# Hybrid attention layer: six x tiles and three blocks of look-ahead in the output stage, a later value product in the local attention, a later request for the next head's bias

## The chip, the cores and the metric

One of the cores of a Trainium2 chip runs the whole kernel. The metric is the device time of one execution in microseconds, the median of three runs. The five engines are TensorE (PE; its weight loads are shown as a lane of their own, PEld), VectorE (DVE), ScalarE (ACT), GpSimd (POOL) and SyncE (SP). In this kernel SP issues every DMA, and it issues them in one order.

## The reference, cut to what matters

Two sequences, 1024 tokens (prompt) and 2048 tokens (sample), width 1024, float32, each go through the same layer:

```python
u = x * (1.0 + scale[:, None]) + shift[:, None]
qa, ka, va, ga, qb, kb, vb, gb = jnp.split(u @ w_in, SPLIT_OFFSETS, axis=-1)
oa = window_gqa(qa, ka, va, sink, rel_bias) * jax.nn.silu(ga)
ob = diff_attention(qb, kb, vb, lq1, lk1, lq2, lk2, subln_w, rel_bias, lambda_init) * jax.nn.silu(gb)
h = jnp.concatenate([oa, ob], axis=-1) @ w_out
return layer_norm(ALPHA * x + gate[:, None] * h, ln_g, ln_b)
```

`window_gqa` is the local attention: 8 heads, blocks of 128 queries, each against its own block of keys and the two beside it, with a bias by distance. `diff_attention` has 4 heads of two softmaxes each over all keys, again with a bias by distance, and takes one from the other.

## The kernel before, in words

A float32 product is made of three matmuls on rounded parts: high by high, high by low, low by high. Most products appear three times in the profile for that reason (L186 to L188, L864 to L866, L1037 to L1039); the local attention's logits and values take two.

The work runs in four stages, one after another on TensorE:

1. **Projections** (to about 669 us): `u` is built and multiplied by `w_in`. The results go to DRAM. A part of this work is kept back and used as filler beside the next stage.
2. **Local attention** (`windowed`, about 669 to 1080 us): 24 blocks, each in two halves `n` of four heads. `first(B, n)` makes the logits of a head per step (matmul L602, bias and minimum on DVE L604, exponential on ACT L607). `second(B, n)` is run two halves later: a step per key block `b`, with four transposes into one PSUM tile (L635), a rounded copy on ACT (`pthA`, L638) and the rest on DVE (`ptlA`, L639). The value product of key block `b` (L629 with `pthA`, L630 with `ptlA`) stands one step behind, right after the transposes of `b + 1`. The last step adds up and stores. A half has four steps, and in each of them, beside a step of `first` and a step of `second`, `beside()` takes some matmuls of the kept-back projections.
3. **Differential attention** (`slot`, about 1098 to 1870 us): units of 128 queries (256 for the prompt) with `logits`, `transpose` three units later, and `values`. The sample's heads have 16 units each. Each head has a bias tile `W` (128x2432), made by `load_head` from one DMA and two spreads on POOL (L752), and key tiles. They come from `Ring`s: buffers that are opened in two steps. For the first three units, while the projections' pool is still open, `W` has one buffer and the keys four; afterwards there are two and six. `prefetch` calls `load_head` for the next head at unit `i == 2` of a head, which for the first head is in the time of the small rings.
4. **Output** (`outputs`, about 1863 us to the end): 24 blocks of 128 tokens, the sample's 16 and then the prompt's 8. `load_rest(t)` asks for five pieces: `ot`, `frow`, `gb` and `oa` into one tile `d` (from `dat`), and the block's `x` (from `xts`). `join(t)` multiplies them (POOL L1006 and L1007) and splits the result in `oH` (ACT L1010) and `oL` (POOL L1011). `output` runs 48 matmuls of 512 columns (L1037 to L1039) into PSUM tiles `po` (four, two per block), then gate, residual and statistics on DVE (L1042 to L1052), the power on POOL (L1053), the scaling on ACT into the `x` tile (L1077), the addition on POOL (L1078), and the store of the `x` tile (L1079). `Views(make, n)` hands out `n` tiles in turn; here 3 for `x`, 2 for `d`, 2 for `oH`/`oL`. All of them are memory of the earlier stage: value tiles `vt`, rows `l`, query tiles `Q` and transposed tiles `pth`/`ptl`.

TensorE's order is the order of the program text (`manual_schedule`). The order on the other engines and on SP is set by a planner, which simulates the kernel and issues what is ready, and what has a free buffer, first. Each engine then keeps its order and waits in place.

Of the kernel before, what the change touches and what calls it, by code (L numbers as in the profile page):

```python
# [11 lines left out]
F32 = mybir.dt.float32  # L12
F32R = mybir.dt.float32r
AF = mybir.ActivationFunctionType
ALU = mybir.AluOpType
# [4 lines left out]
P = 128  # L20
# [46 lines left out]
def hybrid_layer(ctx, tc, x_prompt, x_sample, c_prompt, c_sample, w_in, w_out, w_ada, b_ada, ln_g, ln_b,  # L67
                 attn_sink, lambda_q1, lambda_k1, lambda_q2, lambda_k2, subln_w, rel_bias, oh, eye,
                 y_prompt, y_sample):
    nc = tc.nc  # L70
# [15 lines left out]
    def tp():  # L86
        return ps_tp.tile([P, 512], F32, tag="tp", name="tp")
# [20 lines left out]
    grow = dt_([2, D], "grow")  # L108
# [3 lines left out]
    ident = const.tile([P, P], F32, name="ident")  # L112
# [189 lines left out]
    done, pending = {}, []  # L302
# [230 lines left out]
    def windowed(upto):  # L533

        order = [(s, i) for s in (0, 1) for i in range(SEQS[s] // P)]
        NB = len(order)
        Bs, seconds, n0 = {}, [iter(()), iter(())], done.get(2, 0)
        total = (upto - n0) * 32
        Bs[0] = load_block(*order[0])
        count = [0, 0]  # L540

        def beside():
            count[0] += 1
            while count[1] * NB * 16 < count[0] * total and done.get(2, 0) < upto:
                next(steps, None)
                count[1] += 1

        for t in range(NB + 2):
            for n in range(2):
                if t < NB and order[t][0] == 1 and order[t][1] >= 7:  # L550
                    project_until(2, 5)
                f = first(Bs[t], n) if t < NB else iter(())
                for h4 in range(4):
                    next(f, None)
                    beside()
                    next(seconds[0], None)
                    beside()
                for _ in seconds[0]:
                    pass
                seconds = [seconds[1], second(Bs[t], n) if t < NB else iter(())]  # L560
                if n == 0 and t + 1 < NB:
                    Bs[t + 1] = load_block(*order[t + 1])
            Bs.pop(t - 1, None)
        project_until(2, upto)

    def load_keys_of(s, i):
# [53 lines left out]
    def second(B, n):  # L620

        nb, l = B["nb"], B["l"][n]
        O = ac()
        parts = []

        def values(b):
            H, L = parts[b]
            v = B["V"][:, b, n * P:(n + 1) * P]
            nc.tensor.matmul(O, lhsT=v, rhs=H, start=(b == 0), stop=False)  # L629
            nc.tensor.matmul(O, lhsT=v, rhs=L, start=False, stop=(b == nb - 1))  # L630

        for b in range(nb):
            pt = tp()
            for h4 in range(4):
                nc.tensor.transpose(pt[:, h4 * P:(h4 + 1) * P], l[:, h4, 1 + b * P:1 + (b + 1) * P], ident)  # L635
            H = pa_p.tile([P, 512], F32R, tag="pth", name="pthA")
            L = pa_p.tile([P, 512], F32R, tag="ptl", name="ptlA")
            nc.scalar.copy(H, pt)  # L638
            nc.vector.tensor_tensor(out=L, in0=pt, in1=H.bitcast(F32), op=ALU.subtract)  # L639
            parts.append((H, L))  # L640
            if b:
                values(b - 1)
            yield
        values(nb - 1)
        if n == 0:
            B["og"] = og_p.tile([P, 4, P], F32, tag="og", name="og")
        og = B["og"]
        tmp = og_p.tile([HD, 2, 2, P], F32, tag="tmp", name="tmpA")
        nc.scalar.copy(tmp, O[HD:P, :].rearrange("p (j m q) -> p j m q", j=2, m=2))
        o4 = O[0:HD, :].rearrange("p (j m q) -> p j m q", j=2, m=2)  # L650
        for m in range(2):
            nc.vector.tensor_tensor(out=og[m * HD:(m + 1) * HD, 2 * n:2 * n + 2, :], in0=o4[:, :, m, :],
                                    in1=tmp[:, :, m, :], op=ALU.add)
        if n == 1:
            nc.gpsimd.tensor_tensor(out=og, in0=og, in1=B["G"], op=ALU.mult)
            s, cs = B["s"], slice(B["i"] * P, (B["i"] + 1) * P)
            nc.sync.dma_start(out=OA[s][:, :, cs].rearrange("i r t -> r i t"), in_=og)
        yield
# [10 lines left out]
    pa_p = pool(ast, "ptA", 3)  # L669
# [30 lines left out]
    class Views:  # L700
# [5 lines left out]
        def next(self):  # L706
            if len(self.made) < self.count:
                self.made.append(self.make())
            self.n += 1
            return self.made[(self.n - 1) % self.count]  # L710
# [8 lines left out]
    units, groups_of, values_at, sums_at = [], [], {}, {}  # L719
    for s in (1, 0):  # L720
        T = SEQS[s] // P
        for h in range(HB):
            for i in range(0, T, 2):
                g = len(groups_of)
                n = len(units)
# [7 lines left out]
    order = [(s, h) for s in (1, 0) for h in range(HB)]  # L733
# [41 lines left out]
    def prefetch(n, j):  # L775

        s, h, i, g = units[n]
        if n + 1 < N and j == 1 and g != units[n + 1][3]:
            load_queries(units[n + 1][3])
        if i == 2 and j == 2 and (s, h) != units[-1][:2]:  # L780
            load_head(*next_head[s, h])
        if n + 1 < N and units[n + 1][2] == 0 and j == 3:
            load_keys(*units[n + 1][:2], range(2, SEQS[units[n + 1][0]] // CH))
# [50 lines left out]
    def transpose(n, j):  # L834
# [5 lines left out]
        if b == 0:  # L840
            groups_[g]["PT"].append((pt_p.tile([P, 4, QG], F32R, tag="pth", name="pth"),
                                     pt_p.tile([P, 4, QG], F32R, tag="ptl", name="ptl")))
        H, L = groups_[g]["PT"][kq]
        pt = tp()
# [104 lines left out]
    def part():  # L949
        return weight(next(turn))  # L950
# [4 lines left out]
    def query():  # L955
        return q_p.tile([P, 2, 2, QG], F32R, name="Q").rearrange("p a m q -> p (a m q)")

    def value():
        return v_p.tile([P, 2, 4, P], F32R, tag="v", name="vt").rearrange("p h b e -> p (h b e)")

    os_ = Views(lambda: (query(), query()) if not os_.made else (part(), part()), 2)
    xts = Views(value, 3)
    dat = Views(row0, 2)
    woH, woL, keep, raws = {}, {}, {}, {}

    def stage(ks):
# [21 lines left out]
    def load_rest(t):  # L988

        s, i = order[t]  # L990
        cs = slice(i * P, (i + 1) * P)
        d = dat.next().rearrange("p (n i q) -> p n i q", n=4, i=4)
        nc.sync.dma_start(out=d[:, 1], in_=OT[s][:, :, cs].rearrange("k r t -> r k t"))
        nc.sync.dma_start(out=d[:, 2], in_=frow[s][:, cs].partition_broadcast(P))
        nc.sync.dma_start(out=d[:, 3], in_=GB[s][:, :, cs].rearrange("k r t -> r k t"))
        nc.sync.dma_start(out=d[:, 0], in_=OA[s][:, :, cs].rearrange("i r t -> r i t"))
        xt = xts.next().bitcast(F32)
        nc.sync.dma_start(out=xt, in_=xs[s][cs, :])
        Bs[t] = dict(s=s, i=i, d=d, xt=xt)

    def join(t):

        B = Bs[t]
        d = B["d"]
        B["oH"], B["oL"] = [v.rearrange("p (k q) -> p k q", k=KC) for v in os_.next()]
        nc.gpsimd.tensor_tensor(out=d[:, 1], in0=d[:, 1], in1=d[:, 2], op=ALU.mult)  # L1006
        nc.gpsimd.tensor_tensor(out=d[:, 1], in0=d[:, 1], in1=d[:, 3], op=ALU.mult)  # L1007
        for half in range(2):
            hs = slice(half * 4, half * 4 + 4)
            nc.scalar.copy(B["oH"][:, hs, :], d[:, half])  # L1010
            nc.gpsimd.tensor_tensor(out=B["oL"][:, hs, :], in0=d[:, half], in1=B["oH"][:, hs, :].bitcast(F32),  # L1011
                                    op=ALU.subtract)


    def load_gate(s):
        if "gate" not in keep:
            keep["gate"] = part().bitcast(F32)
        nc.sync.dma_start(out=keep["gate"], in_=grow[s, :].partition_broadcast(P))

    def load_norm():  # L1020
        for name, v in (("g", ln_g), ("b", ln_b)):
# [3 lines left out]
    def output(B, end):  # L1025

        s, cs = B["s"], slice(B["i"] * P, (B["i"] + 1) * P)
        gate, gbc, bbc = keep["gate"], keep["g"], keep["b"]
        xt, oH, oL = B["xt"], B["oH"], B["oL"]
        bs = sA_p.tile([P, 4, 6], F32, tag="bs", name="bs")  # L1030
        accs = []
# [49 lines left out]
    order = [(s, i) for s in (1, 0) for i in range(SEQS[s] // P)]  # L1081
    NB = len(order)
    Bs = {}

    def outputs():

        load_rest(0)
        stage((4, 5, 6, 7))
        yield
        for k in range(3):  # L1090
            split_weights(k)
            yield
        load_gate(order[0][0])
        load_norm()
        for k in range(3, 7):
            split_weights(k)
            yield
        split_weights(7)
        load_rest(1)
        join(0)  # L1100
        for t in range(NB):
            s, i = order[t]
            if i == 0 and t:
                load_gate(s)
            for j, _ in enumerate(output(Bs[t], t == NB - 1)):
                if j == 2 and t + 2 < NB:
                    load_rest(t + 2)
                if j == 8 and t + 1 < NB:
                    join(t + 1)
                yield  # L1110
            del Bs[t]
            yield
# [40 lines left out]
```

## Time and profile before

| what | value |
|---|---|
| median of 3 runs (lowest to highest) | 2234.81 us (2233.54 to 2236.45) |
| the profiled execution | 2232.28 us, its span 2230.5 us |
| mean granted TensorE clock | 0.981 of 2.4 GHz |
| TensorE busy, weight loads busy | 94%, 80% of the span |
| DVE, ACT, POOL busy | 59%, 46%, 52% |
| DMA, mean over the span | 140 GB/s |

The shares are means over stages that have different limits. The table shows TensorE nearly always busy; what can still change must be looked for stage by stage, in the time between one matmul's start and the next. "Idle before" in the rows below is the time in which an engine had nothing, and behind the arrow stands what ended it. PEclk is the granted clock as a share of 2.4 GHz.

### The profile page before, as it was taken

How to read it: one execution, taken by the hardware profiler on the slowest of the kernel's cores; microseconds unless marked ns; L12 is line 12 of the kernel's file. 1: busy time of each engine (PE TensorE's matmuls, PEld its weight loads, DVE VectorE, ACT ScalarE, POOL GpSimd, SP SyncE). 2: the span in 40 equal slices, each digit the busy share in tenths (PEclk: the TensorE clock that was granted, in tenths of full speed). 3: DMA queues.
4: the chain of work that ended last, by engine and by line, in shares of the span. 5: the costliest groups of instructions: out<-in, count | busy, mean ns of one | idle time of the engine just before them, and what ended most of it. 6: DMA issues, size and time to landing. Idle time of an engine off the chain costs nothing.

```text
span 2230.5 us, 32729 instructions
## 1 busy us (share of the span) xinstructions
PE 2104.7 (94%) x11597; PEld 1791.7 (80%) x11597; DVE 1307.5 (59%) x2538; ACT 1031.8 (46%) x2022; POOL 1153.5 (52%) x836
## 2 busy tenths in 40 slices
PE   7999999999999999999999999999999988678898
PEld 4777888888988788888978889999998877556676
DVE  6334124212246667667539889999999975333445
ACT  5211113111136666667327777777778973111111
POOL 3213123212133334433248878888988885455565
PEclk9999999999999999999999999999999998889999
DMA  9676536345359667786524221232315548444553
GB/s 276 179 264 178 158 128 183 114 132 146 129 164 241 162 168 190 192 220 156 155 77 130 78 74 39 79 82 78 76 44 128 114 100 162 97 131 135 151 178 113
DMA packets 340203, 312.46 MB, mean 140 GB/s; under 512 B 32086, under 2 KB 296950, under 8 KB 339656
## 3 DMA queue, kind: packets, MB, share of 16 engines
q1 hardware_dynamic: 340040, 310.37, 51.4%
q8 instruction: 92, 1.51, 0.4%
q14 instruction: 71, 0.58, 0.2%
HBM read 212.70 MB, written 97.60 MB: 139 GB/s over the span
## 4 chain that ended last, share of the span: by engine, by line
PE 41%; DMA 8%; issue 6%; POOL 4%; DVE 2%; ACT 1%; SPq 1%; POOLq 0%; DVEq 0%; ACTq 0%
PE lg L808 12%; PE tp L846 5%; PE ac L866 3%; PE ac L865 3%; PE ac L864 3%; DMA l<-ot 3%; PE pj L186 3%; PE pj L188 3%; PE pj L187 3%; DMA out<-vt 2%; DMA Q<-qb 2%; PE lgA L602 2%; PE tp L635 1%; PE ac L630 1%; POOL vt L1078 1%
## 5 line engine op out<-in xcount | busy, mean ns | idle before, releaser
L186 PE MATMUL pj<-uH,wH 128*128 128x512 f32 x1040 | 415.3, 399 | 5.3 <-DVE gg L257 5.3
L188 PE MATMUL pj<-uH,wL 128*128 128x512 f32 x1040 | 407.8, 392 | 0.0
L187 PE MATMUL pj<-uL,wH 128*128 128x512 f32 x1040 | 407.1, 391 | 0.0
L217 POOL TENSOR_TENSOR wL<-wr,wH 128x1024 fp32r<-128x1024 f32 x74 | 181.6, 2456 | 417.8 <-DVE wH L215 369.9
L808 PE MATMUL lg<-kt,Q 128*128 128x512 f32 x1280 | 380.0, 418 | 14.7 <-DVE nm L813 6.3
L832 POOL TENSOR_TENSOR l<-l,l 128x1024 f32<-128x1024 f32 x160 | 382.4, 2412 | 0.2
L821 ACT ACTIVATE l<-l,nm 128x2048 f32<-128x2048 f32 (+1 forms) x192 | 331.0, 1724 | 26.3 <-DVE nm L813 26.1
L808 PEld LDWEIGHTS lg<-kt,Q 128*128 128x128 f32 x1280 | 218.8, 191 | 48.2 <-issue 10.4
L813 DVE CUSTOM_DVE_ANT_0 l<-lg,W 128x1024 f32<-128x1024 f32 x192 | 233.3, 1215 | 21.2 <-PE lg L808 16.6
L830 POOL TENSOR_SCALAR l<-l,s 128x1024 f32<-128x1024 f32 x160 | 179.1, 1131 | 121.5 <-DVE s L826 52.3
L848 ACT CAST pth<-tp 128x512 fp32r<-128x512 f32 x320 | 186.1, 582 | 118.7 <-PE tp L846 115.0
L188 PEld LDWEIGHTS pj<-uH,wL 128*128 128x128 f32 x1040 | 195.7, 188 | 42.7
L186 PEld LDWEIGHTS pj<-uH,wH 128*128 128x128 f32 x1040 | 195.9, 188 | 38.5 <-DVE gg L257 6.1
L187 PEld LDWEIGHTS pj<-uL,wH 128*128 128x128 f32 x1040 | 196.0, 188 | 31.4
L849 DVE TENSOR_TENSOR ptl<-tp,pth 128x512 fp32r<-128x512 f32 x320 | 209.0, 684 | 16.9 <-ACT pth L848 15.7
L846 PE MATMUL tp<-ident,l 128*128 128x128 f32 x1280 | 195.5, 276 | 9.6 <-DVE ptl L849 9.5
L617 POOL TENSOR_SCALAR l<-l,rcA 128x384 f32<-128x384 f32 (+1 forms) x144 | 82.6, 592 | 202.8 <-DVE rcA L611 179.4
L864 PE MATMUL ac<-pth,vt 128*128 128x256 f32 x640 | 182.1, 285 | 2.9 <-ACT ac L881 2.9
L866 PE MATMUL ac<-pth,vt 128*128 128x256 f32 x640 | 183.1, 286 | 0.0
L865 PE MATMUL ac<-ptl,vt 128*128 128x256 f32 x640 | 182.5, 285 | 0.0
L813 DVE CUSTOM_DVE_ANT_0 l<-lg,W,nm 128x1024 f32<-128x1024 f32 x128 | 164.0, 1281 | 23.2 <-PE lg L808 16.1
L846 PEld LDWEIGHTS tp<-ident,l 128*128 128x128 f32 x1280 | 150.4, 142 | 12.6 <-DVE ptl L849 4.7
(206 smaller groups left out, 4071.7 us busy)
## 6 DMA issues: line engine op xcount, KB each, us to landing
wr<-in_w_in SPq DMA_DIRECT2D x39, 1024.0 KB, 5.6
KAt<-ka SPq DMA_DIRECT2D x40, 384.0 KB, 7.3
QAt<-qa SPq DMA_DIRECT2D x24, 512.0 KB, 5.6
kt<-kb SPq DMA_DIRECT2D x24, 512.0 KB, 6.6
Q<-qb SPq DMA_DIRECT2D x48, 256.0 KB, 3.2
Q<-qb SPq DMA_DIRECT2D x96, 128.0 KB, 4.0
vt<-vb SPq DMA_DIRECT2D x48, 256.0 KB, 6.9
out<-vt SPq DMA_DIRECT2D x23, 512.0 KB, 5.2
```

The source lines that it names most:

```text
L186: nc.tensor.matmul(acc, lhsT=a(k), rhs=b(k), start=(k == 0), stop=False)
L187: nc.tensor.matmul(acc, lhsT=a(k), rhs=bl(k), start=False, stop=False)
L188: nc.tensor.matmul(acc, lhsT=al(k), rhs=b(k), start=False, stop=(k == KC - 1))
L808: nc.tensor.matmul(L[:, c * CH:(c + 1) * CH], lhsT=G["Q"][:, v, m, b * P:(b + 1) * P], rhs=Kt[kt0 + c][:, m, :], start=(v == 0), stop=(v = ...
L813: nc.vector.tensor_tensor_reduce(out=half, in0=L, in1=W[:, off:off + 1024], scale=1.0, scalar=nm[:, m, 0:1] if s and hf else 3e38, op0=ALU ...
L821: nc.scalar.activation(e, e, AF.Exp, bias=nm[:, m, hf:hf + 1], scale=-1.0, accum_out=sums)
L832: nc.gpsimd.tensor_tensor(out=row[:, cs], in0=row[:, cs], in1=rows[n][1][:, cs], op=ALU.add)
L846: nc.tensor.transpose(pt[:, c * P:(c + 1) * P], rows[n][0][:, (j * 4 + c) * P:(j * 4 + c + 1) * P], ident)
L849: nc.vector.tensor_tensor(out=L[:, :, qs], in0=p3, in1=H[:, :, qs].bitcast(F32), op=ALU.subtract)
L864: nc.tensor.matmul(a, lhsT=Vt[kq][:, 0, c, :], rhs=H[:, c, :], start=(kb == 0), stop=False)
L865: nc.tensor.matmul(a, lhsT=Vt[kq][:, 0, c, :], rhs=L[:, c, :], start=False, stop=False)
L866: nc.tensor.matmul(a, lhsT=Vt[kq][:, 1, c, :], rhs=H[:, c, :], start=False, stop=(kb == T - 1))
```

## The change

Four edits in the output stage: six tiles for `x` instead of three, four for `d` instead of two, three pairs of `oH`/`oL` instead of two; `load_rest` runs three blocks ahead instead of two, and `join` is called at step 4 of the block before instead of step 8; the gate vectors of the two sequences get a tile each, and the second is asked for at block 8 instead of being loaded over the first at block 16. In the local attention the value product of key block `b` stands in front of the transposes of `b + 2`, so `second` has one more step than a half has, and two halves' generators can be alive at once. In the differential attention the next head is asked for at `i == 4` instead of 2 in the sample's heads.

```diff
-        Bs, seconds, n0 = {}, [iter(()), iter(())], done.get(2, 0)
+        Bs, live, wait, n0 = {}, [], [], done.get(2, 0)
@@ windowed
-                    next(seconds[0], None)
+                    for g in list(live):
+                        if next(g, live) is live:
+                            live.remove(g)
                     beside()
-                for _ in seconds[0]:
-                    pass
-                seconds = [seconds[1], second(Bs[t], n) if t < NB else iter(())]
+                if t < NB:
+                    wait.append(second(Bs[t], n))
+                if len(wait) > 1 or t >= NB and wait:
+                    live.append(wait.pop(0))
@@ second
-        for b in range(nb):
-            pt = tp()
...
-            if b:
-                values(b - 1)
-            yield
-        values(nb - 1)
+        for b in range(nb + 2):
+            if b > 1:
+                values(b - 2)
+            if b < nb:
+                pt = tp()
...
+            if b <= nb:
+                yield
@@ prefetch
-        if i == 2 and j == 2 and (s, h) != units[-1][:2]:
+        if i == (4 if s else 2) and j == 2 and (s, h) != units[-1][:2]:
             load_head(*next_head[s, h])
@@
-    os_ = Views(lambda: (query(), query()) if not os_.made else (part(), part()), 2)
-    xts = Views(value, 3)
-    dat = Views(row0, 2)
+    os_ = Views(lambda: (query(), query()) if not os_.made else (part(), part()), 3)
+    xts = Views(lambda: value() if len(xts.made) < 5 else part(), 6)
+    dat = Views(row0, 4)
@@ load_gate
-        if "gate" not in keep:
-            keep["gate"] = part().bitcast(F32)
-        nc.sync.dma_start(out=keep["gate"], in_=grow[s, :].partition_broadcast(P))
+        keep[s] = part().bitcast(F32)
+        nc.sync.dma_start(out=keep[s], in_=grow[s, :].partition_broadcast(P))
@@ outputs
         load_rest(1)
+        load_rest(2)
         join(0)
         for t in range(NB):
-            s, i = order[t]
-            if i == 0 and t:
-                load_gate(s)
+            if t == 8:
+                load_gate(0)
             for j, _ in enumerate(output(Bs[t], t == NB - 1)):
-                if j == 2 and t + 2 < NB:
-                    load_rest(t + 2)
-                if j == 8 and t + 1 < NB:
+                if j == 2 and t + 3 < NB:
+                    load_rest(t + 3)
+                if j == 4 and t + 1 < NB:
                     join(t + 1)
```

## Rows read from the trace of the kernel before

**Rows 1.** Busy time of the engines in stretches of the span: the local attention, the first head change, the entry to the output stage, its first 16 blocks and the later ones. Columns: length; busy us (instructions) of PE, PEld, DVE, ACT, POOL; granted clock; DMA share; GB/s.
```profile
669.00:1080.00 411.00, 398.71 (x2116) 330.40 (x2115) 278.40 (x719) 272.87 (x698) 153.37 (x185) 1.00 0.73 186
...
1165.00:1300.00 135.00, 125.28 (x805) 111.65 (x806) 115.84 (x219) 96.62 (x155) 103.26 (x65) 0.97 0.34 97
...
1833.00:1884.30 51.30, 39.97 (x241) 36.19 (x240) 31.04 (x52) 23.87 (x64) 31.98 (x25) 0.87 0.75 168
1884.30:2122.00 237.70, 183.79 (x720) 144.05 (x719) 88.15 (x150) 32.70 (x57) 117.01 (x105) 0.91 0.49 127
2122.00:2211.30 89.30, 82.56 (x339) 65.15 (x338) 40.83 (x70) 17.33 (x30) 58.07 (x51) 0.96 0.50 163
```

**Rows 2.** Who waited for whom from 1884.3 to 2211.3 us (blocks 1 to 22 of the output). Columns: who, for whom, us in total, times, the longest.
```profile
ACT vt L1077 <- POOL ve L1053: 272.6, 22, 19.7
...
POOL l L1006 <- DMA l<-ot: 147.2, 21, 14.1
...
PE po L1037 <- ACT vt L1077: 60.5, 18, 8.9
```

**Rows 3.** The same stretch, what SP's queue itself waited for (L998 loads x, L994 loads frow).
```profile
SPq L994 <- POOL l L1006: 111.5, 19, 11.1
...
SPq L998 <- DMA out<-vt: 51.8, 19, 5.7
```

**Rows 4.** POOL in order of time over one block. Columns: start, us, engine, line, operation, out<-in, count, idle before.
```profile
2043.51 1.29 POOL L1006 TENSOR_TENSOR l<-l 128x512 f32<-128x512 f32 x1 [7.58 <-DMA l<-ot]
2044.77 2.53 POOL L1078 TENSOR_TENSOR vt<-vt,pth 128x512 f32<-128x512 f32 x2
...
2058.66 1.28 POOL L1006 TENSOR_TENSOR l<-l 128x512 f32<-128x512 f32 x1 [7.14 <-DMA l<-ot]
```

**Rows 5.** SP's queue in order of time in the same block: the store, the x load and the ot load.
```profile
2047.32 0.35 SPq L1079 DMA_DIRECT2D out<-vt  x1
...
2054.08 0.35 SPq L998 DMA_DIRECT2D vt<-in_x_sample  x1
2054.52 0.39 SPq L993 DMA_DIRECT2D l<-ot  x1
```

**Rows 6.** TensorE in order of time: the first matmul of blocks 1, 22 and 23 of the output.
```profile
1884.32 0.39 PE L1037 MATMUL po<-kt,ptl 128*128 128x512 f32 x1
...
2200.15 0.50 PE L1037 MATMUL po<-kt,Q 128*128 128x512 f32 x1
...
2211.32 0.39 PE L1037 MATMUL po<-kt,ptl 128*128 128x512 f32 x1
```

**Rows 7.** Busy time in three shorter stretches: the wait ahead of block 2, blocks 17 and 18, block 22. Columns as in rows 1.
```profile
1884.30:1910.00 25.70, 17.47 (x68) 13.77 (x67) 9.66 (x17) 2.91 (x5) 6.81 (x8) 0.87 0.55 60
...
2137.00:2159.90 22.90, 22.70 (x98) 17.95 (x96) 13.54 (x23) 3.81 (x7) 13.93 (x12) 1.00 0.53 173
...
2200.00:2211.00 11.00, 10.87 (x48) 8.89 (x48) 5.88 (x10) 2.98 (x6) 8.09 (x7) 1.00 0.42 155
```

**Rows 8.** Who waited for whom from 669 to 1080 us, TensorE's rows.
```profile
PEld ac L630 <- DVE ptlA L639: 22.3, 55, 1.1
...
PE ac L630 <- DVE ptlA L639: 6.3, 15, 0.7
...
PEld ac L629 <- ACT pthA L638: 4.0, 5, 2.0
...
PE ac L629 <- ACT pthA L638: 2.8, 4, 1.8
...
PE tp L635 <- DVE ptlA L639: 1.4, 2, 0.7
```

**Rows 9.** TensorE in order of time in the local attention: the transposes of two key blocks that follow each other, and the value product of the first of them.
```profile
1000.35 0.60 PE L635 MATMUL tp<-ident,l 128*128 128x128 f32 x4
...
1002.55 0.60 PE L635 MATMUL tp<-ident,l 128*128 128x128 f32 x4
1002.90 0.47 PE L629 MATMUL ac<-pthA,VAt 128*128 128x512 f32 x1
```

**Rows 10.** What SP's queue waited for from 669 to 1080 us, the row of the load of G (L587).
```profile
SPq L587 <- POOL og L655: 37.6, 15, 8.7
```

**Rows 11.** TensorE in order of time at the change from the sample's first head to its second: the logits of consecutive rounds (a round is four logits matmuls, six of values, four transposes).
```profile
1268.99 1.17 PE L808 MATMUL lg<-kt,Q 128*128 128x512 f32 x4
...
1271.08 1.18 PE L808 MATMUL lg<-kt,Q 128*128 128x512 f32 x4
...
1273.85 0.71 PE L808 MATMUL lg<-kt,Q 128*128 128x512 f32 x2 [0.44 <-DMA kt<-kb]
...
1276.69 1.17 PE L808 MATMUL lg<-kt,Q 128*128 128x512 f32 x4
...
1284.82 2.04 PE L808 MATMUL lg<-kt,Q 128*128 128x512 f32 x4 [5.81 <-DVE nm L813]
...
1288.65 1.63 PE L808 MATMUL lg<-kt,Q 128*128 128x512 f32 x4
...
1291.19 1.17 PE L808 MATMUL lg<-kt,Q 128*128 128x512 f32 x4
```

**Rows 12.** SP's queue there: the load of the second head's W.
```profile
1274.08 0.54 SPq L750 DMA_DIRECT2D W<-tbl  x1
```

**Rows 13.** POOL there: the spreading of that W.
```profile
1281.35 2.06 POOL L752 TENSOR_SCALAR W<-W 128x1024 f32<-128x1024 f32 x2 [2.71 <-DMA W<-tbl]
```

More of the change, by code (lines that the diff above doesn't have):

```diff
@@ L555, in windowed @@
                     beside()
-                    next(seconds[0], None)
+                    for g in list(live):
+                        if next(g, live) is live:
+                            live.remove(g)
                     beside()
-                for _ in seconds[0]:
-                    pass
-                seconds = [seconds[1], second(Bs[t], n) if t < NB else iter(())]
+                if t < NB:
+                    wait.append(second(Bs[t], n))
+                if len(wait) > 1 or t >= NB and wait:
+                    live.append(wait.pop(0))
                 if n == 0 and t + 1 < NB:
                     Bs[t + 1] = load_block(*order[t + 1])
-            Bs.pop(t - 1, None)
+        for g in live:
+            for _ in g:
+                pass
         project_until(2, upto)
@@ L630, in values @@
             nc.tensor.matmul(O, lhsT=v, rhs=L, start=False, stop=(b == nb - 1))
-        for b in range(nb):
-            pt = tp()
[L634 to L640, printed above, removed]
-            if b:
-                values(b - 1)
-            yield
-        values(nb - 1)
+        for b in range(nb + 2):
[3 more added lines that the diff above has]
+                pt = tp()
+                for h4 in range(4):
+                    nc.tensor.transpose(pt[:, h4 * P:(h4 + 1) * P], l[:, h4, 1 + b * P:1 + (b + 1) * P], ident)
+                H = pa_p.tile([P, 512], F32R, tag="pth", name="pthA")
+                L = pa_p.tile([P, 512], F32R, tag="ptl", name="ptlA")
+                nc.scalar.copy(H, pt)
+                nc.vector.tensor_tensor(out=L, in0=pt, in1=H.bitcast(F32), op=ALU.subtract)
+                parts.append((H, L))
+            if b <= nb:
+                yield
         if n == 0:
@@ L1027, in output @@
         s, cs = B["s"], slice(B["i"] * P, (B["i"] + 1) * P)
-        gate, gbc, bbc = keep["gate"], keep["g"], keep["b"]
+        gate, gbc, bbc = keep[s], keep["g"], keep["b"]
         xt, oH, oL = B["xt"], B["oH"], B["oL"]
@@ L1092, in outputs @@
             yield
-        load_gate(order[0][0])
+        load_gate(1)
         load_norm()
```

## The prediction

> **What bounds the kernel now.** I read the busy table first: TensorE 94%. So I looked next for stretches in which that share is lower, by windows over the stages [rows 1]. From 669 to 1080 us TensorE is busy 398.7 of 411 us; around the first head change 125.3 of 135; in the output 183.8 of 237.7 and then 82.6 of 89.3. No other engine comes near its limit in the output: DVE has 129.0 and POOL 175.1 us of work in 327 [rows 1]. So the output waits for something, and the question is what ends last.
>
> The waits of that stretch name POOL: L1006, the first multiplication of `join`, waited 147.2 us for the `ot` load, 21 times, so 7.0 each; TensorE's 60.5 us follow from it, since `oH` comes last in that chain (the row names ACT's L1077, which stands in front of the `oH` copies on ACT) [rows 2]. The load is late because SP is held: its x load waited 51.8 us in 19 places for a store of the same x tile [rows 3]. One turn of the loop can be read off: L1006 at 2043.51, L1078 at 2044.77 for 2.53, store issued at 2047.32, x load only at 2054.08, `ot` behind it at 2054.52, and L1006 again at 2058.66, which is 15.15 us [rows 4, 5]. The blocks run at that pace: from block 1's first matmul (1884.32) to block 23's (2211.32) lie 22 blocks in 327.0 us, 14.86 each [rows 6].
>
> **The change, part by part.**
>
> *Output.* With six x tiles the x load of block t+3 goes into the tile of t-3, stored long before; with four `d` tiles its loads wait for a join that is long done. That removes both waits of SP [rows 3], and with them the loop. What is late next? TensorE itself. Block 22, for which everything lay ready, took 2211.32 - 2200.15 = 11.17 us [rows 6]; blocks 17 and 18 took 22.9 us together at clock 1.00, 11.45 each, with joins, loads and stores going on [rows 7]. POOL needs 175.1 / 22 = 8.0 us per block and DVE 129.0 / 22 = 5.9 [rows 1], both below 11.2. I take 11.45, since those blocks carry all the traffic: 22 x (14.86 - 11.45) = 75.0 us. The ends are 81 (11.17) and 49: the later blocks made 339 matmuls, 7.06 blocks of 48, in 89.3 us, 12.65 each [rows 1], and 22 x 2.21 = 49.
> Against it stands the entry. Four blocks' loads now want to come where two did, while the DMA share is already 0.75 from 1833 on [rows 1]. The wait ahead of block 2 is there today, 25.7 - 17.5 = 8.2 us [rows 7]; I leave half of it, 4 us (ends 0 and 8). A gate tile of its own, the third `oH`/`oL` pair and `join` at step 4 add no instruction; they cost nothing as long as their memory (transposed tiles of the last groups) is free by then: in the program text the last groups' products stand beside block 0, ahead of block 1. The output gives 75 - 4 = 71.
>
> How much headroom a TensorE stage has depends on the measure. By matmul busy time the 327 us hold 266.35 us of work [rows 1], so 60.7 would be the most that can go. By starts it is 81, because half of the loss sits inside busy time: the granted clock was 0.91 over the first 16 blocks, a mixture of 2.4 and 1.2 GHz, and 1.00 in block 22 [rows 1, 7]. The Trainium skill (Perfetto Trace Analysis, Identifying the Most-Contended Engine) says that matmul busy time is a poor measure and that the share of weight loads should be used. By it the stretch stands at 209.2 / 327.0 = 64% and block 22 at 8.89 / 11.0 = 81%, so 327 x (1 - 0.64 / 0.81) = 68 us could go and the total below would be about 10 higher. A weight load at the lower clock counts as work there, so I stay with the starts.
>
> *Local attention.* The matmuls of the low part (L630) waited for DVE's `ptlA`, 55 times as a weight load for 22.3 us and 15 times as a matmul for 6.3; L629 waited 4.0 and 2.8 for ACT [rows 8]. A weight load that comes late delays its matmul; both lanes show one stall between them, so the loss lies between 6.3 + 2.8 = 9.1 and 22.3 + 4.0 = 26.3. Today the transposes of a key block start at 1000.35 and its product at 1002.90, 2.55 us later, in steps of 2.20 [rows 9]. After the change two steps lie between, 4.4 us. The 1.85 us gained exceed the longest common wait (1.1); only one of 2.0 is longer [rows 8]. No instruction is added, and the three `pthA`/`ptlA` buffers suffice, as the product of b now stands in front of the copy for b + 2. Late next: the same transposes need the PSUM tile that the same DVE instruction frees, 1.4 us today [rows 8]. On the other side, `second` ends a step later, and G's load holds SP until then: 37.6 us in 15 waits today [rows 10], up to 15 x 2.2 = 33 more. Stores and weight loads queue behind it, but TensorE hardly waits for those now. I take the middle of the two upper figures, 18 us; the ends are 26 and a loss of 33.
>
> *Next head's bias.* For the first head `i == 2` falls into the time when `W` has one buffer, so the second head's `W` could be asked for only when the first was finished with it: issued at 1274.08 [rows 12], spread by POOL from 1281.35 to 1283.41 [rows 13], and TensorE idle 5.8 us behind it. A round of logits takes 2.09 us; the five rounds from 1271.08 to 1291.19 took 20.11 instead of 10.45, so 9.7 us were lost [rows 11], part of it after the gap at a lower clock (the stretch has 0.97 [rows 1]). At `i == 4` the second buffer exists, eleven units before it is needed. The 1.4 us before the gap belong to late keys [rows 11], and two of the four key tiles still come at the change. I take 8 (ends 0 and 9.7). The other heads' requests move by two units and are hidden either way; POOL spreads as often as before.
>
> *Sum.* 71 + 18 + 8 = 97. The profiled execution took 2232.28, so its like would take 2135.3; the median of the runs shown is 2.5 above that execution, and against it I expect 2234.8 - 97 = 2138 us.
>
> **Rivals.**
>
> *A, the output stops at 12.65 us a block.* POOL's order is the planner's: a join set behind L1078 of the block before, or loads set behind a store, leaves a short gap and a low clock at many block starts, as in the later blocks today. For it: those blocks had shorter waits and still did not reach 11.2 [rows 1]. Against: blocks 17 and 18 did, with two tiles [rows 7]. 2234.8 - 49 - 26 = 2160.
>
> *B, the local stall only moves* to the PSUM tile of the transposes or to SP behind G's load. For it: one DVE instruction ends both waits [rows 8], and SP is held there [rows 10]. Against: that event now has 1.85 us more. Without the 18 us: 2156; with a loss of 15, half of the 33, 2171.
>
> *C, slower: look-ahead lost on SP and POOL.* SP and POOL each wait in place. If the planner sets the joins in front of L1078 and the load that the next block needs still behind the store, all of POOL's 8.0 us per block enter the loop (today L1006 and L1078 do, 3.8 of them), and with the 11.3 from store to L1006 [rows 4, 5] a block takes 19.3: 22 x (19.3 - 14.86) = 98 more, less 26 from the other parts, gives 2307. It makes the kernel slower from 14.86 + 26 / 22 = 16.0 us a block on. For it: SP already waited 111.5 us for POOL's L1006 [rows 3]. Against: with four `d` and six x tiles the planner has no reason to set a load that late.
>
> *D, more than the sum:* all three at their upper ends, 81 + 26 + 9.7 = 117, gives 2118.
>
> **How the numbers follow.** The forecast has 0.60, with 2122 to 2154 as its own range; A 0.20, B 0.12, C 0.04, D 0.04. Together the three edits have to lose their gain before the time is the same; that leaves 0.94 for faster by over 0.2% (4.5 us, about what these runs can tell), 0.02 for within it, 0.04 for slower. The range of 8 in 10 takes in A and B without loss and stops ahead of C: 2114 to 2168.
>
> **What would show it.** In the output: x loads that no longer wait for stores, no wait of L1006 for `ot`, L1037 at a start every 11.2 to 11.6 us, and a clock of 1.00. If L1006 still waits but for `frow`, A is at work. In the local attention: the L630 and L629 waits gone, and not returned as L635 waiting for `ptlA` or as waits for weights. At the first head change: the second head's `W` issued long before the first head ends, and no gap. The prediction is wrong if block starts lie 12.6 us or more apart, or if SP's wait for G grows and TensorE's busy share from 669 to 1080 us does not.

## The result, and the profile after

The changed kernel takes 2200.9 us, median of 4 runs (2195.32 to 2202.11); the kernel before took 2235.0 beside it. The ratio is 0.9843 [0.9825, 0.9861]: faster by 34 us (1.6%), where 97 were forecast. The profiled execution took 2195.32 us, its span 2193.5.

Lines have moved: `join` is now L1012, L1013 (POOL), L1016 (ACT), L1017 (POOL); the power L1058, scaling L1082, addition L1083, store L1084; the loads of ot, frow, gb, oa and x L999, L1000, L1001, L1002, L1004; the output's matmuls L1042 to L1044. In experiments with added lines these are one or two higher.

Read by TensorE's first matmul of each stage, the 37.0 us between the two spans come from:

| stage | before | after |
|---|---|---|
| start to the first local logits | 669.6 | 666.1 |
| local attention | 428.3 | 412.6 |
| differential attention, first to last logits | 735.4 | 725.3 |
| last logits to the output's first matmul | 29.8 | 32.1 |
| output's first matmul to the end | 367.4 | 357.5 |

The local attention and the head change gave 15.7 and 10.1 us, about what was forecast (18 and 8). The output gave 9.9 instead of 71. So the question is the output.

First the busy time in stretches of the changed kernel, as in [rows 1]: local attention, entry, blocks 1 to 16, blocks 17 to 22.

```profile
666.00:1078.00 412.00, 405.27 (x2257) 345.29 (x2257) 277.50 (x725) 276.92 (x701) 160.51 (x190) 1.00 0.76 197
1804.00:1863.40 59.40, 41.65 (x241) 37.36 (x240) 30.94 (x50) 22.77 (x59) 32.09 (x26) 0.83 0.64 157
1863.40:2106.80 243.40, 192.97 (x770) 151.61 (x769) 94.25 (x162) 38.49 (x71) 137.12 (x121) 0.90 0.58 155
2106.80:2174.30 67.50, 67.22 (x290) 53.89 (x289) 35.25 (x60) 12.84 (x21) 38.58 (x34) 1.00 0.25 91
```

The last six blocks, for which all loads had been asked for long before, took 67.5 us, 11.25 each, at clock 1.00. The sixteen before them took 243.4, 15.2 each, at 0.90.

The waits of POOL, of ACT, of SP's queue and of TensorE from 1836 us on (columns: who, for whom, us in total, times, longest):

```profile
POOL l L1012 <- DMA l<-ot: 110.6, 20, 17.5
...
ACT vt L1082 <- POOL ve L1058: 191.5, 16, 32.9
...
SPq L1084 <- POOL vt L1083: 91.2, 18, 10.7
SPq L1000 <- POOL l L1012: 69.4, 12, 9.0
SPq L1004 <- DMA out<-vt: 24.4, 10, 6.7
...
PE po L1042 <- ACT vt L1082: 47.1, 11, 23.8
```

SP waits less for a store (L1004; 51.8 us before [rows 3]), as forecast, though it still does. But POOL still waits in place for `ot`, 20 times instead of 21, 110.6 us instead of 147.2 [rows 2]. With loads three blocks ahead it should not. POOL in order of time shows why (columns as in [rows 4]):

```profile
2046.67 1.28 POOL L1012 TENSOR_TENSOR l<-l 128x512 f32<-128x512 f32 x1 [5.13 <-DMA l<-ot]
2047.91 2.54 POOL L1083 TENSOR_TENSOR vt<-vt,pth 128x512 f32<-128x512 f32 x2
2050.41 1.28 POOL L1013 TENSOR_TENSOR l<-l 128x512 f32<-128x512 f32 x1
2051.65 2.52 POOL L1017 TENSOR_TENSOR pth<-l,ptl 128x512 fp32r<-128x512 f32 x2
2054.12 0.55 POOL L1058 TENSOR_TENSOR ve<-ve,mhalf 128x1 f32<-128x1 f32 x1
2058.86 1.29 POOL L1012 TENSOR_TENSOR l<-l 128x512 f32<-128x512 f32 x1 [4.19 <-DMA l<-ot]
```

Counted from the first, the L1012 at 2046.67 is block 17's, and TensorE starts block 17 at 2106.8, 60 us later. The two L1083 right behind it are block 10's: the join of a block seven later stands in front of them. Before, the L1006 at 2058.66 [rows 4] was block 13's, whose matmuls began at 2085.3, 26.6 us later, and it stood in front of block 9's additions, four back. The loads were asked for earlier, and POOL's order set the multiplication earlier too, right at the load. POOL waits there for a value that nobody wants for four blocks, and behind it stand the additions of a finished block (so its store and SP), the subtraction (L1017) that ends the join of block 14 and the power (L1058, so ACT's L1082 and the PSUM tile that TensorE needs).

The wait also feeds itself. The `ot` load of block 18 goes into the row tile of block 14 (row tiles are the `d` tiles, now four), so SP can issue it only behind that L1017, and the L1012 at 2058.86 waits for it. SP's `ot` loads of blocks 17 and 18:

```profile
2041.22 0.37 SPq L999 DMA_DIRECT2D l<-ot  x1
2054.46 0.39 SPq L999 DMA_DIRECT2D l<-ot  x1
```

From one to the next is 13.24 us, a turn of this loop. From block 11 on, SP issues every `ot` load within 1.6 us of the end of the last L1017 of the block four earlier.

At the entry the same thing costs most. POOL, ACT and TensorE around block 3 of the changed kernel:

```profile
1875.03 0.56 POOL L1058 TENSOR_TENSOR ve<-ve,mhalf 128x1 f32<-128x1 f32 x1
1893.14 1.26 POOL L1012 TENSOR_TENSOR l<-l 128x512 f32<-128x512 f32 x1 [17.55 <-DMA l<-ot]
...
1906.16 1.26 POOL L1012 TENSOR_TENSOR l<-l 128x512 f32<-128x512 f32 x1 [6.89 <-DMA l<-ot]
...
1910.27 0.55 POOL L1058 TENSOR_TENSOR ve<-ve,mhalf 128x1 f32<-128x1 f32 x1
```

```profile
1910.85 1.26 ACT L1082 ACTIVATE vt<-po,ve 128x512 f32<-128x512 f32 x2 [32.94 <-POOL ve L1058]
```

```profile
1911.59 0.80 PE L1042 MATMUL po<-kt,Q 128*128 128x512 f32 x1 [23.84 <-ACT vt L1082]
```

The first matmul of block 3 waited 23.84 us for a PSUM tile of block 1. Block 1's power, the L1058 at 1910.27, is one instruction of 0.55 us, and it stood behind the first multiplications of blocks 5, 6 and 7 (the one at 1875.03 is block 0's).

### The profile page after: what moved, and what is told of

Its sections match the earlier page's. It is cut to its first block, busy times and chain, and to the rows that moved or that the text cites. A ratio compares the mean times of both kernels' runs of the same rounds, so it can differ in the third digit from the quotient of the medians.

```text
span 2193.5 us, 32703 instructions
## 1 busy us (share of the span) xinstructions
PE 2081.7 (95%) x11597; PEld 1781.9 (81%) x11597; DVE 1300.9 (59%) x2538; ACT 1034.6 (47%) x2022; POOL 1153.6 (53%) x836
## 4 chain that ended last, share of the span: by engine, by line
PE 74%; DMA 11%; POOL 5%; issue 4%; DVE 3%; SPq 2%; ACT 1%; DVEq 0%; POOLq 0%; ACTq 0%
PE lg L814 13%; PE pj L186 11%; PE pj L187 11%; PE pj L188 11%; PE tp L852 6%; PE ac L872 3%; PE ac L871 3%; PE ac L870 3%; PE lgA L607 3%; PE tp L643 2%; DMA l<-ot 2%; PE ac L635 2%; DMA Q<-qb 1%; PE po L1042 1%; PE ac L634 1%
```

## The experiments

My theory after the result is that POOL's order is the bound, since `join` stands in it too early for its load. The rivals: the loads themselves are too slow; the store and the x load on SP are still the loop; the output edits simply have nothing to give. Each time stands beside runs of the kernel before on the same chip (2224 to 2231 us). Pitch is the distance of block 23's first matmul from block 1's, over 22.

| run | median, us | ratio to before | first output matmul to end | pitch |
|---|---|---|---|---|
| before | 2234.8 | 1 | 367.4 | 14.86 |
| changed | 2200.9 | 0.9843 [0.9825, 0.9861] | 357.5 | 14.13 |
| e1 no output edits | 2207.2 | 0.9913 [0.9894, 0.9932] | 363.2 | 14.67 |
| e2 join behind the power | 2143.5 | 0.9653 [0.9626, 0.9679] | 306.5 | 11.99 |
| e3 the same, two ahead | 2135.8 | 0.9594 [0.9572, 0.9617] | 297.5 | 11.40 |
| e4 two row tiles (not the layer's result, see below) | 2203.0 | 0.9902 [0.9882, 0.9923] | 363.7 | 13.67 |
| e5 order without depth | 2137.2 | 0.9587 [0.9571, 0.9604] | 303.5 | 11.95 |
| e6 output edits alone | 2215.9 | 0.9939 [0.9925, 0.9953] | 355.5 | 14.02 |
| e7 local attention alone | 2209.5 | 0.9922 [0.9901, 0.9943] | 360.6 | 14.55 |
| e8 next head alone | 2216.9 | 0.9945 [0.9931, 0.9959] | 362.3 | 14.63 |
| e9 e2 with x behind a later store | 2126.5 | 0.9535 [0.9513, 0.9557] | 288.9 | 11.11 |
| e10 e3 with the same | 2129.4 | 0.9553 [0.9530, 0.9577] | 289.9 | 11.11 |
| e11 x order alone | 2186.5 | 0.9807 [0.9782, 0.9832] | 347.9 | 13.60 |

### The parts alone: e1, e6, e7, e8

e1 is the changed kernel with the output stage of before; e6, e7 and e8 are the kernel before with one part of the change each, as its diff shows them.

> The changed kernel with the output stage of before (three x tiles, loads two blocks ahead, one gate tile, join at the eighth step); the edits of local attention and of the next head's bias stay. My theory: those two give 16 + 10 us, and the output edits only some 8, because in the changed kernel POOL stands in place at L1012 for loads that nobody needs yet. So 2207 to 2211 us, the changed kernel 0.995 to 0.997 of it. Rival (the output edits do give some 70 us, and the loss is elsewhere): about 2270 us. Rival (the output edits give nothing or cost): 2200 us or less.

> The kernel before with the output edits alone. My theory (the output edits gain some 0.7% as e1 says, 8 to 15 us, because the waits in place on POOL take the rest): ratio 0.992 to 0.997. Rival (the output edits gain less beside the other two edits than alone): ratio below 0.985.

> The kernel before with the edit of local attention alone. By the two profiles the stage lost 15.7 us of its 428: ratio 0.992 to 0.994. Rival (half of it comes back as waits further on): 0.996 to 0.998.

> The kernel before with the next head's bias asked for at the later place alone. The wait of some 8 us at the head change goes and nothing else moves: ratio 0.996 to 0.997. Rival (the load is only moved, and the next head waits for it): 0.999 to 1.001.

The output edits alone gain 0.61%, 13.6 us of 2228, the local attention 17.4, the next head 12.3. The first two came as expected, the third better than that. e1 has the expected 2207, but on a chip on which the kernel before took 2224, so it gains less than expected (19 us, not 26); against it the changed kernel stands at 0.9843 / 0.9913 = 0.993 (0.995 to 0.997 expected), so the rivals of 70 us and of nothing both fall. Together the three parts gain less (1.57%) than alone (1.94%), and e1 gains 19 us where e7 and e8 add up to 30. That difference stays open.

### The order on POOL: e2 and e3

```diff
-        nc.gpsimd.tensor_tensor(out=ve[:, 1:2], ..., op=ALU.pow)
+        powers[B["n"]] = nc.gpsimd.tensor_tensor(out=ve[:, 1:2], ..., op=ALU.pow).ins
...
                 if j == 4 and t + 1 < NB:
-                    join(t + 1)
+                    with tc.issue_after(powers[t - 1]) if t else ExitStack():
+                        join(t + 1)
```

`issue_after` makes the planner set `join`'s POOL instructions behind the named one, which is POOL's too. In e3 it is `join(t + 2)`, with `join(1)` ahead of the loop.

> The changed kernel, with the join of block t+1 queued on POOL behind the power (L1058) of block t-1, and still called at the fourth step of block t; loads, tiles and everything else as changed. My theory (POOL waiting in place at L1012 for the ot load of a block four ahead is what holds the output): the 23.8 us wait at block 3 goes, the pitch of the output blocks falls from about 13 to 11.3 to 12 us, and the time to 2150 to 2175 us. Rival (the loads themselves are too slow with three blocks in flight): the pitch stays at 13, PE's waits are for loads, 2190 to 2205 us. Rival (a join this late is itself on the path, its five POOL instructions and two copies come after the block that needs them): slower than 2205 us.

> As the run before, but in block t the join of block t+2 is the one that is queued behind the power of block t-1 (block 1 is joined before the loop). It gives each join a block more of lead and each load a block less. My theory: no wait in place on POOL, joins a block early, pitch 11.1 to 11.6 us, 2140 to 2165 us. Rival (loads too slow): pitch about 13, and now POOL waits at L1012 again, 2190 to 2205 us.

Both came out where the theory had them or lower (some 10 us of that is the chip, on which the kernel before took 2224 too). e2 is 1.9% faster than the changed kernel by the two ratios, e3 2.5%, with the same loads and the same tiles; the output stage fell by 51 and 60 us. What is left of POOL's waits for `ot` in e3, from 1843 us on:

```profile
POOL l L1012 <- DMA l<-ot: 1.8, 2, 1.4
```

In the changed kernel it was 110.6 us in 20 waits. So the loads are not too slow, and the late join costs nothing that outweighs this.

### Is the depth needed at all? e5, and a run that did not test it, e4

```diff
                 if j == 8 and t + 1 < NB:
-                    join(t + 1)
+                    with tc.issue_after(powers[t - 1]) if t else ExitStack():
+                        join(t + 1)
```

e5 is e1 with the order alone: three x tiles, two row tiles, loads two blocks ahead.

> Local attention and head bias as changed, the output stage of before (three x tiles, two row tiles, loads two blocks ahead, join at the eighth step), with only the join of block t+1 queued on POOL behind the power of block t-1, as in e2. It tells how much of e2's gain is the queue order alone. If the order alone is what matters: pitch 12.5, 2145 to 2160 us. If the depth of the loads is needed as well (my view: with two row tiles the ot load of block t+2 can only go out after the join of block t, and each load took some 5 us from its issue until the join could use it): pitch 13.5 to 15, 2175 to 2205 us.

My view was wrong, the other branch right, and better than its figure: 2137.2 us, as good as e3 with about twice the tiles. One order is worth 3.3% against e1, 73 us by the two ratios. POOL over part of a block of e1, where block 9's L1012 waits in front of the additions of block 5, whose power is the line above:

```profile
1963.07 0.55 POOL L1059 TENSOR_TENSOR ve<-ve,mhalf 128x1 f32<-128x1 f32 x1
1971.02 1.29 POOL L1012 TENSOR_TENSOR l<-l 128x512 f32<-128x512 f32 x1 [7.40 <-DMA l<-ot]
1972.27 2.55 POOL L1084 TENSOR_TENSOR vt<-vt,pth 128x512 f32<-128x512 f32 x2
```

and of e5, where the power and the addition are block 9's, and block 11's L1012 between them, 7.6 us ahead of its block's first matmul (1977.2), finds its data there:

```profile
1969.07 0.55 POOL L1059 TENSOR_TENSOR ve<-ve,mhalf 128x1 f32<-128x1 f32 x1
1969.59 1.29 POOL L1012 TENSOR_TENSOR l<-l 128x512 f32<-128x512 f32 x1
1970.83 1.29 POOL L1017 TENSOR_TENSOR pth<-l,ptl 128x512 fp32r<-128x512 f32 x1
1972.08 1.29 POOL L1084 TENSOR_TENSOR vt<-vt,pth 128x512 f32<-128x512 f32 x1
```

POOL's wait for `ot`, first of e1 (from 1843 to 2133 us), then of e5:

```profile
POOL l L1012 <- DMA l<-ot: 128.2, 18, 13.3
```

```profile
POOL l L1012 <- DMA l<-ot: 1.6, 2, 1.2
```

The planner sets SP's order anew for each kernel, so e5 does not leave SP untouched: SP's wait for L1012 ahead of the `frow` load fell from 110.5 us in e1 to 5.1, and no run has POOL's new order with SP's old one. But SP's x load waits more there than in e1, and the blocks are faster all the same. First e1, then e5:

```profile
SPq L1004 <- DMA out<-vt: 45.8, 15, 4.7
```

```profile
SPq L1004 <- DMA out<-vt: 112.4, 21, 7.6
```

So the x load's wait for a store, which the prediction took for the loop, was not what set 14.7 us.

e4 is the changed kernel with `dat = Views(row0, 2)`.

> The changed kernel with two row tiles in dat instead of four (the size of before), everything else as changed: a block's ot can then only be loaded when the block two before it is split, so L1012 can't stand more than two blocks early on POOL. My theory: the block 3 wait of 23.8 us goes (it came from L1012 of blocks 5, 6 and 7 ahead of the power of block 1), the pitch is 12 to 14 us since the loads have less lead; 2180 to 2205 us, so no slower than the changed kernel. Rival (the deeper row tiles are what gives the changed kernel its gain): pitch back at 14.8 us, 2205 to 2215 us.

It tells little: with two tiles the load of block t+3, which stands ahead of the join of block t+1 in the program, takes that block's tile, so that each of these joins works on the rows of a later block and waits for a later load; what it computes is no longer the layer. POOL waited 111.6 us for `ot` in it. Its time, no better than the changed kernel's, says nothing on the theory.

### What bounds next: e9, e10, e11

In e2 the pitch was 12.0, not 11.1. SP's queue over one block of e2:

```profile
1945.89 0.34 SPq L1004 DMA_DIRECT2D vt<-in_x_sample  x1
...
1947.91 1.81 SPq L1084 DMA_DIRECT2D out<-ptl  x1
1949.81 2.60 SPq L999 DMA_DIRECT2D l<-ot  x1
1958.70 0.34 SPq L1004 DMA_DIRECT2D ptl<-in_x_sample  x1
```

The x load at 1958.70 goes into the tile of the store at 1947.91 and waits for it to land. The next store stands behind that x load. The loop that I had seen before the change is there after all, now with six tiles: SP's order lets each x load follow the store of its own tile, 12.81 us from x load to x load here. e9 and e10 set the x load behind a later store:

```diff
-        nc.sync.dma_start(out=xt, in_=xs[s][cs, :])
+        with tc.issue_after(stores[t - 4]) if t - 4 in stores else ExitStack():
+            nc.sync.dma_start(out=xt, in_=xs[s][cs, :])
...
-        nc.sync.dma_start(out=ys[s][cs, :], in_=xt)
+        stores[B["n"]] = nc.sync.dma_start(out=ys[s][cs, :], in_=xt).ins
```

> e2 (join behind the power) with one more order: the x load of block t+3 is queued on SP behind the store of block t-1, where e2 queues it behind the store of block t-3, whose tile it takes, and so waits with everything else of SP's for that store to land (L1004 waits 115 us in 18 times for out). Theory: this loop of store, landing, x load, next store sets e2's pitch of 12.5 us; without it the pitch is 11.1 to 11.5 us, 2110 to 2130 us. Rival (the transfers themselves, 2 MB a block, set 12.5 us): the pitch stays, 2138 to 2148 us.

> e3 (join two blocks ahead) with the same order of the x loads. Theory: blocks 13 to 16, which had 12.6 to 14 us in e3, go to 11.1 to 11.5 us; 2110 to 2128 us. Rival (transfers): as e3, 2130 to 2140 us.

> The changed kernel with the order of the x loads alone, the joins left where they are. If POOL's order is the first bound and the store loop only the next one: the pitch stays about 13 us and the wait at block 3 stays, 2190 to 2205 us. Rival (the store loop is the common cause, and POOL only waits because SP is late): 2140 to 2165 us.

In e9 and e10 each of the blocks 1 to 22 takes 11.11 us. The rival (transfers of 2 MB a block as the limit) falls. e10, a little above its 2110 to 2128, is no better than e9: in its profiled execution the output starts 8.4 us later, but all of that is lost ahead of the last logits, and its block 0 takes 26.0 us against 25.0. Why the stages ahead are longer there stays open. Busy time of e9 from block 1 to block 23, and below it SP there:

```profile
1860.80:2105.30 244.50, 244.50 (x1057) 198.17 (x1056) 129.49 (x222) 54.08 (x91) 178.41 (x155) 1.00 0.64 177
```

```profile
1959.90 5.47 SPq L1085 DMA_DIRECT2D out<-vt  x1
1965.42 0.42 SPq L1005 DMA_DIRECT2D vt<-in_x_sample  x1
1965.94 1.44 SPq L999 DMA_DIRECT2D l<-ot  x1
...
1970.69 4.49 SPq L1085 DMA_DIRECT2D out<-vt  x1
1975.24 0.43 SPq L1005 DMA_DIRECT2D vt<-in_x_sample  x1
```

TensorE is busy 244.50 of 244.50 us at clock 1.00, and the x load no longer waits. e11, the same order in the changed kernel without the order of the joins, came out at 2186.5, a little below the 2190 to 2205 expected of the first theory and far from the rival's 2140 to 2165. POOL's wait is still there:

```profile
POOL l L1013 <- DMA l<-ot: 96.6, 18, 11.5
```

So there are two loops, one behind the other. POOL's order is the first, worth 3.3% (e1 to e5); SP's x order is worth 0.4% with it left (changed to e11, intervals that overlap). Once it is gone, it is worth about 1.2% with the join one block ahead (e2 to e9) and 0.4% with the join two ahead (e3 to e10, intervals that overlap).

## Why the prediction was right or wrong

*What bounds the output.* Half right. TensorE waits for something, L1006 waits for `ot`, and TensorE itself would be next: all true, and the size too. The link between the two was read wrongly. The prediction has `oH` come last and sets the row that names ACT's L1077 aside; the row was right. ACT and TensorE of the kernel before, at the start of block 11:

```profile
2051.55 1.26 ACT L1077 ACTIVATE vt<-po,ve 128x512 f32<-128x512 f32 x2 [13.29 <-POOL ve L1053]
...
2052.29 0.50 PE L1037 MATMUL po<-kt,ptl 128*128 128x512 f32 x1 [2.67 <-ACT vt L1077]
```

TensorE waited for the PSUM tile of block 9, ACT's scaling for block 9's power, and that power stood on POOL behind the L1006 of block 12. By starts the prediction gave 81 us as the most that can go; e9 got 22 x (14.86 - 11.11) = 82.5. The Trainium skill (Perfetto Trace Analysis, Identifying the Most-Contended Engine) has TensorE's headroom judged by its share of the peak arithmetic rate and by the share of weight loads; from the second the prediction estimated 68 us. That share describes e9 correctly (198.17 / 244.50 = 81%, as in the block taken as reference), but the 68 were too few, because weight loads at the lower clock count as work: from block 1 to 22 of the kernel before, a weight load took 0.33 us where the granted clock was 1.2 GHz and 0.19 where it was 2.4. That half of the loss sits inside busy time is a slip: of the 81 us, 60.7 are idle time, so it is a quarter.

*The step that failed* is "with four `d` tiles its loads wait for a join that is long done. That removes both waits of SP [rows 3], and with them the loop." The waits only shrank: for the store from 51.8 to 28.5 us (24.4 of it for `vt` tiles), for POOL's L1006 or L1012 from 111.5 to 69.4. The join was not long done: the `ot` load of block 18 went out 0.3 us behind the last L1017 of block 14. The loop ran on through POOL: L1012 went up in POOL's order with its load, from 26.6 to 60.1 us ahead of its block and from four to seven blocks ahead of the additions behind it, and still waited in place. The prediction read a POOL instruction that waits as a load that is late. It was as much an instruction that is early: e5, with the tiles and the look-ahead of before, gains as much as e3. The 71 us of this term measured 9.9 between the two profiles and 13.6 alone (e6).

*The entry.* Taken at 4 us, between 0 and 8; a single wait of 23.84 us at block 3. The prediction asked for the DMA share there, not for what stands in front of block 1's power on POOL.

*Local attention.* 18 forecast; 15.7 by the profiles, 17.4 alone (e7). The size came out, the reasoning only in part: all waits of L630 and L629 should have gone, and about half did. TensorE's waits from 670 to 1051 us, and those of its weight loads from 666 to 1079 us:

```profile
PE ac L635 <- DVE ptlA L647: 3.3, 7, 1.0
PE tp L643 <- DVE ptlA L647: 2.9, 3, 1.4
```

```profile
PEld ac L635 <- DVE ptlA L647: 13.6, 37, 1.3
```

L635 (the old L630) still waits, 13.6 us as weight loads instead of 22.3, and 3.3 as matmuls instead of 6.3 [rows 8]; the claim that 1.85 us more exceed every common wait was too neat. The 18 was the middle of two bounds for the loss of all these waits; that it fits when half of them went is partly luck. The transposes' wait for the PSUM tile grew from 1.4 to 2.9, a small part of rival B. The feared loss on SP did not come: its wait for G's load was 38.5 us in 13 places against 37.6 in 15 [rows 10].

*Next head's bias.* Right; 8 forecast, 10.1 between the profiles, 7.0 in e8's stage and 12.3 by e8's runs. SP's request and the spread of the second head's `W`, then TensorE's logits from the last round of the first head on:

```profile
1155.61 0.64 SPq L756 DMA_DIRECT2D W<-tbl  x1
```

```profile
1163.93 2.06 POOL L758 TENSOR_SCALAR W<-W 128x1024 f32<-128x1024 f32 x2 [2.80 <-DMA W<-tbl]
```

```profile
1251.85 1.18 PE L814 MATMUL lg<-kt,Q 128*128 128x512 f32 x4
1253.93 1.17 PE L814 MATMUL lg<-kt,Q 128*128 128x512 f32 x4
1256.00 1.18 PE L814 MATMUL lg<-kt,Q 128*128 128x512 f32 x4
1258.08 1.17 PE L814 MATMUL lg<-kt,Q 128*128 128x512 f32 x4
```

The `W` is there some 88 us before the second head's first logits at 1253.93, and the rounds go on every 2.1 us with no gap. The five rounds that took 20.11 us [rows 11] take 10.4.

*Rivals.* A comes nearest by its price and its clock below 1.00, but its order is the other way round: it has a join behind the addition of the block before, and in the trace the joins stand ahead of additions. Its price, 12.65 us a block, was read from the later blocks; the changed kernel needed 14.13. The case against A, that blocks 17 and 18 took 11.45 us each, was misread: from start to start they took 11.5 and 14.1, since block 19 began only at 2162.9, outside the stretch that was measured. C had named the place (joins ahead of the addition on POOL), but the second half of its condition did not hold: the load that the next block needs was there in time. The prediction's argument against it, "the planner has no reason to set a load that late", looked at loads only; the damage was that it set joins that early. The forecast's own sign of failure, block starts 12.6 us or more apart, is what the profile shows.

## What to carry to other kernels

When an engine waits in place for a load, look at two distances: how late the load was asked for, and how long before its use the waiting instruction stands in its engine's order. More buffers and a longer look-ahead help only if the order of the consumers does not move up with the loads; here fixing the consumer behind the last thing that must not wait gave 73 us with no buffer at all. When one loop is gone, look for the next in the same queues: a load that follows the store of its own tile, with other stores behind it, set the next bound.

## What was not expected of the hardware

The instruction that issues a store on SP took 0.35 us in the changed kernel (at 2050.47), and 3.9 to 8.7 us for the first ten stores of e9 (4.49 and 5.47 in the lines above); from 1992 us on it took 0.35 or less in e9 too. The rate of the DMA is not the reason: it moved 190 GB/s from 1860.8 to 1976 us, while the issues were long, and 197 from 1982 to 2050, while they were short. What sets them stays open. In e9 they cost nothing, since TensorE waited for nothing from block 1 to block 23. And the waits cost twice, as idle time and in the granted clock: 0.90 over blocks 1 to 16 of the changed kernel, a mean of 1.2 and 2.4 GHz, and 1.00 in e9 once the waits were gone.
